# Layer 0's expert products in tiles of 32 columns throughout

## The chip, the core and the metric

The kernel runs on one core of a Trainium2 chip. A core has five engines with queues of their own: TensorE (PE in the profile; its weight loads stand apart as PEld) multiplies matrices into PSUM, VectorE (DVE), ScalarE (ACT) and GpSimd (POOL) compute element by element, and SyncE (SP) issues transfers. Sixteen DMA engines move data between device memory and the core. Engines wait for each other by semaphores alone. The metric is the device time of one execution in microseconds.

TensorE holds a stationary operand of up to 128 rows and 128 columns and streams a moving operand past it. Where the stationary operand has only 64 or 32 columns, two or four products that write different column stretches (here: different partitions of a PSUM bank) can stand side by side in the array.

## The reference

A backbone of two layers over 256 latent and 256 context tokens of width 1024. Each layer has a token mixer and then a mixture of experts, all in fp32. What matters here is the mixture of layer 0, which all 512 tokens pass: each token goes to 2 of 16 experts.

```python
out = jnp.zeros((T, D), F32)
for e in range(N_EXPERTS):
    y = (jax.nn.silu(h @ w1[e]) * (h @ w3[e])) @ w2[e]
    out = out + combine[:, e:e + 1] * y
```

`w1` and `w3` are 1024 x 512, `w2` is 512 x 1024; an expert's weights are 6.3 MB in fp32.

## The kernel before

The kernel goes through layer 0's mixer, its routing, its experts (the function `all0` inside `experts`), then layer 1's mixer and experts. The change is in `all0` alone.

An expert has room for 96 tokens (`cap`). The tokens are the stationary operand, the weights are the moving one, 512 columns at a time. The 96 are cut into `ab`, the first 64, and `cc`, the last 32.

- `hidden(e, q)` (lines 872 to 888), q = 0 to 3, multiplies a quarter of the model width, two slices of 128 (`i`), with the matching pieces of `w3` and `w1` (`j`). For the 64 tokens it issues four matmuls of 64 columns into the bank `A` (tile `h` in the profile): j = 0 goes to partitions 0 to 63, j = 1 to 64 to 127. For the 32 tokens it issues four matmuls of 32 columns into the bank `C` (`hc`), one for each pair of `i` and `j`; the two `i` are added later by `both_halves`.
- `middle(e)` (lines 896 to 910) makes the gated hidden values `gg` on ScalarE and VectorE: it copies and adds the halves of `hc` (lines 893, 894, tile `gs`), takes silu (901, 902) and multiplies (905, or 907 for the last two experts).
- Four transposes on TensorE (line 219, tile `gT`) and a copy on ScalarE (1007) turn `gg`.
- `down(e, gT)` (lines 912 to 933) multiplies with `w2`, 128 rows a piece, in two groups `g` of two pieces: four matmuls of 64 columns into the bank `y[0]`, then four of 32 into `y[1]`. Experts 14 and 15 take another branch, with 96 columns.
- `turn_rows` transposes the gathered tokens of a later expert (tile `xt`), and `aside()` slips in small pieces of routing work (some of them with matmuls `sw`).

The order of TensorE is written out by hand: `in_line` gives each matmul an order token, and the loop over `e` places hidden(e+1, 0) between `middle(e)` and the transposes `gT`, hidden(e+1, 1) and `down(e)` behind them, then `xt`, hidden(e+1, 2), `xt`, hidden(e+1, 3). ScalarE and VectorE keep the order of the tokens named "moe". So all three run in program order.

The weights come on SyncE's queue in the order of use (`stream`), through a ring of 30 buffers of 512 KB (`slots`); a piece is issued when the piece that had its buffer has been used (lines 202 and 863). After expert 11's iteration `without(late)` takes out the buffers that later work needs, and ten are left. Tokens are fetched, and results stored to `yD`, over GpSimd's queue. When expert 13 is stored, GpSimd gathers the results of experts 0 to 13 by token (`room`, line 1063), and `fetched` adds them up. The last two experts are added by a matmul. Behind the weights of the last expert SyncE's queue has layer 1's first weights, `in_od_w_in`.

Of the kernel before, what the change touches and what calls it, by code (L numbers as in the profile page):

```python
# [135 lines left out]
def tile_kernel(ctx: ExitStack, tc: tile.TileContext, I, out, stage=99, dbg=None):  # L136
# [48 lines left out]
    def ps(nm, tag="ps"):  # L185
        tag = alias.get(tag, tag)
        pp, n = psums.get(tag) or psums["ps"]
        return pp.tile([P, 512], F32, tag=tag if tag in psums else "ps", name=nm, bufs=n)
# [18 lines left out]
    def inorder(inst, name="last"):  # L207

        tc.stamp_issue_order_token(inst.ins, name)
# [3 lines left out]
    def mm(*args, **kw):  # L213
        inst = nc.tensor.matmul(*args, **kw)  # L214
        if in_line[0]:
            inorder(inst, "line")
# [233 lines left out]
    def moe(l, tiles, cap, ng, x1, pm, pn, hhi=None, hlo=None):  # L450
# [182 lines left out]
        def experts(pe, ysb, rest, spare=None, next_norm=None):  # L633
# [117 lines left out]
            XTe, xe, idt = {}, {}, {}  # L751
# [60 lines left out]
            def all0(rest):  # L812
# [54 lines left out]
                def weights(e, u):  # L867
                    load(place[e, u] + 3)
                    return loaded[e, u]

                hs = {}
                ab, cc = slice(0, 64), slice(64, 96)

                def hidden(e, q):


                    if q == 0:
                        hs[e] = ps("h", "h"), ps("hc", "h")
                    w = [weights(e, u) for u in (ups[q][1], ups[q][0])]
                    A, C = hs[e]  # L880
                    for i in range(2):
                        for j in range(2):
                            mm(A[64 * j:64 * j + 64, :], XTe[e][:, 2 * q + i, ab], w[j][:, i], start=(q + i == 0),
                               stop=(q + i == 4))
                    for i in range(2):
                        for j in range(2):
                            r0 = 64 * i + 32 * j
                            mm(C[r0:r0 + 32, :], XTe[e][:, 2 * q + i, cc], w[j][:, i], start=(q == 0), stop=(q == 3))
# [22 lines left out]
                def down(e, gT):  # L911


                    y = [ps("y", "y") for _ in range(2)]
                    if e > 13:
                        for f in range(4):
                            w = weights(e, 8 + f)
                            for h in range(2):
                                mm(y[h][r], gT[:, f], w[:, h], start=(f == 0), stop=(f == 3))
                        return y  # L920
                    for g in range(2):
                        ws = [weights(e, 8 + 2 * g + i) for i in range(2)]
                        for i in range(2):
                            for h in range(2):
                                mm(y[0][64 * h:64 * h + 64, :], gT[:, 2 * g + i, ab], ws[i][:, h], start=(g + i == 0),
                                   stop=(g + i == 2))
                        for i in range(2):
                            for h in range(2):
                                r0 = 64 * i + 32 * h
                                mm(y[1][r0:r0 + 32, :], gT[:, 2 * g + i, cc], ws[i][:, h], start=(g == 0), stop=(g == 1))  # L930
                    return y
# [49 lines left out]
                for h in range(2):  # L981
                    turn_rows(0, h)
                hidden(0, 0)
                side.append(one_hot0(2, 4, BF16, put))
                turn_rows(1, 0)
                hidden(0, 1)
                turn_rows(1, 1)
                for _ in range(5):
                    aside()
                hidden(0, 2)  # L990
                side.append(ids(2, 4, put))
                for _ in range(2):
# [5 lines left out]
                for e in range(16):  # L998
# [7 lines left out]
                    gT = pe.tile([P, 4, cap], F32, tag="gT", name="gT", bufs=2)  # L1006
# [3 lines left out]
                    else:  # L1010
                        for n in (2, 3):
                            fetched(n, put)
                    y = down(e, gT)
                    if e < 14:
                        o = ysb[:, e % 2, :]
# [492 lines left out]
    with ExitStack() as es:  # L1508
# [237 lines left out]
        for kh in range(2):  # L1746
            w = cp.tile([P, 4, 512], F32R, tag=f"x{kh + 3}", name="wc")
# [79 lines left out]
    with ExitStack() as es:  # L1827
# [81 lines left out]
        for qt in range(2):  # L1909
            qs = slice(qt * 128, qt * 128 + 128)  # L1910
            ob = pA.tile([P, 512], F32, tag="ob", name="ob", bufs=2)
            for h in range(4):
# [18 lines left out]
                for k in range(4):  # L1931
                    mm(oacc[:, 0:128], wT[:, k, :], dv[:, k, h * 128:(h + 1) * 128],
                       start=(k == 0), stop=(k == 3))
# [23 lines left out]
    with tc.tile_pool(name="pT", bufs=1) as pT:  # L1957

        for q in range(4):
            pTs = []  # L1960
            for hp in range(2):
                h = 2 * q + hp
# [20 lines left out]
            for qt in range(2):  # L1983
                for k in range(4):
                    for hp in range(2):
                        mm(acc_o[64 * hp:64 * hp + 64, qt * 128:qt * 128 + 128],
                           nv[:, k, (2 * q + hp) * 64:(2 * q + hp) * 64 + 64], pTs[hp][:, qt, k, :],
                           start=(k == 0), stop=(k == 3))
# [63 lines left out]
```

## Time and profile before

| | us |
|---|---|
| median of 3 runs | 1437.96 |
| lowest and highest run | 1434.01, 1445.67 |
| the profiled execution's own time | 1443.12 |
| its span, first to last instruction | 1441.1 |
| TensorE busy in it | 1267.0 (88%) |
| VectorE, ScalarE, GpSimd busy | 590.1, 425.6, 218.1 |
| bytes moved | 349.22 MB, 242 GB/s on the mean |

The profile is of one execution. Busy time is the time in which an engine had an instruction of the program in work; matmuls overlap in their pipeline, so a busy TensorE can still have time to give. An fp32 matmul shows as two weight loads and two matmul instructions, and the trace counts each. A row of the timeline joins neighbouring instructions of one kind: start, length from the first start to the last end, count. "PEclk" is the granted share of TensorE's full clock. The DMA share is the mean busy share of the 16 engines; it can read a little over 1.

### The profile page before, as it was taken

Reading aid. Unit: us, or ns where it says so; the run is one execution under the profiler, and the core shown is the slowest. Engines: PE = TensorE matmul, PEld = TensorE weight load, DVE = VectorE, ACT = ScalarE, POOL = GpSimd, SP = SyncE. Lnnn points to the kernel's source line nnn. Section 1 sums busy time; section 2 is a strip of 40 time slices with the busy share of each in tenths; the row PEclk is TensorE's granted clock in tenths of the full one; section 3 lists DMA queues with packets and bytes.
Section 4 is the critical chain, followed back from the end, with each engine's and each line's share of the span. In section 5 each row is a group of like instructions: output and inputs, shape, how many; then the busy total and the mean of one; then the engine's idle time right before and its main releaser. Section 6 shows DMA issues by size and latency. Waiting matters only on the chain. (4 is left out here: it accounts for less than half of the span.)

```text
span 1441.1 us, 22145 instructions
## 1 busy us (share of the span) xinstructions
PE 1267.0 (88%) x8700; PEld 687.0 (48%) x8700; DVE 590.1 (41%) x1329; ACT 425.6 (30%) x835; POOL 218.1 (15%) x271
## 2 busy tenths in 40 slices
PE   5999778888989886999999987799998699999975
PEld 0556556666756672222222223776766544433321
DVE  1326846778656632222112238744636611110003
ACT  2753322222223321221222123324637321111102
POOL 0005520333411301111111120310000100000000
PEclk9999989989999967999999996799999799999998
DMA  9687677766783757999998790651442679999554
GB/s 335 209 256 216 179 181 203 174 172 177 183 262 129 248 221 275 369 383 383 380 382 304 256 365 23 147 139 59 146 169 88 208 265 398 400 396 395 222 223 172
DMA packets 240320, 349.22 MB, mean 242 GB/s; under 512 B 96120, under 2 KB 126104, under 8 KB 239952
## 3 DMA queue, kind: packets, MB, share of 16 engines
q1 hardware_dynamic: 226240, 304.72, 62.9%
q0 software_dynamic: 11264, 34.72, 7.4%
q10 hardware_dynamic: 2704, 8.27, 1.6%
q8 instruction: 72, 1.18, 0.3%
q14 instruction: 40, 0.33, 0.1%
HBM read 326.86 MB, written 20.79 MB: 241 GB/s over the span
## 5 line engine op out<-in xcount | busy, mean ns | idle before, releaser
L214 PE MATMUL y<-w,gT 128*64 128x512 f32 (+2 forms) x736 | 163.0, 612 | 2.1 <-ACT gT L698 1.5
L214 PE MATMUL pj<-hh,whi 128*128 128x512 f32 x432 | 150.1, 429 | 0.6 <-ACT hh L224 0.3
L214 PE MATMUL h<-w,XT 128*64 128x512 f32 x512 | 138.6, 614 | 5.1 <-issue 5.1
L224 DVE TENSOR_TENSOR wlo<-w,whi 128x512 fp32r<-128x512 f32 (+1 forms) x104 | 84.7, 828 | 111.5 <-ACT whi L224 107.4
L214 PE MATMUL h<-w,XE 128*64 128x512 f32 x512 | 125.4, 611 | 3.0 <-ACT XE L790 2.5
L224 ACT ACTIVATE whi<-w 128x512 fp32r<-128x512 f32 (+1 forms) x104 | 69.9, 700 | 155.4 <-DMA w<-in_ev_w_in_dram 73.0
L214 PEld LDWEIGHTS pj<-hh,whi 128*128 128x128 f32 x432 | 83.6, 202 | 32.4 <-issue 9.8
L214 PEld LDWEIGHTS y<-w,gT 128*64 128x64 f32 (+2 forms) x736 | 44.9, 131 | 101.7 <-issue 91.4
L214 PE MATMUL pj<-hh,wlo 128*128 128x512 f32 x216 | 89.9, 418 | 2.1 <-DVE wlo L224 2.0
L214 PE MATMUL ada<-w,sT 128*32 128x512 f32 x384 | 69.0, 639 | 16.9 <-DMA w<-in_ada_w_dram 10.0
L214 PE MATMUL hc<-w,XE 128*32 128x512 f32 x512 | 68.2, 605 | 0.1
L214 PEld LDWEIGHTS h<-w,XT 128*64 128x64 f32 x512 | 36.4, 138 | 63.6 <-issue 57.6
L894 DVE TENSOR_TENSOR ysb<-y,ysb 64x512 f32<-64x512 f32 x14 | 9.7, 695 | 139.1 <-ACT ysb L893 139.1
L214 PEld LDWEIGHTS h<-w,XE 128*64 128x64 f32 x512 | 31.3, 137 | 57.1 <-issue 48.1
L806 DVE SCALAR_TENSOR_TENSOR ylo<-y,sw,yhi 128x512 fp32r<-128x512 f32 x16 | 12.0, 751 | 100.7 <-ACT yhi L805 100.7
L214 PEld LDWEIGHTS pj<-hh,wlo 128*128 128x128 f32 x216 | 43.5, 201 | 17.0 <-DVE wlo L224 4.7
L689 DVE TENSOR_TENSOR gg<-gg,h 64x512 f32<-64x512 f32 x16 | 11.1, 691 | 95.0 <-ACT gg L688 95.0
L2024 POOL TENSOR_TENSOR x<-x,fg 128x512 f32<-128x512 f32 x2 | 2.8, 1378 | 284.9 <-ACT sq L2023 284.9
L1020 POOL DMA_DIRECT2D yD<-ysb x28 | 15.1, 545 | 171.7 <-ACT ysb L1016 171.7
L1016 ACT ACTIVATE ysb<-y 128x512 f32<-128x512 f32 x14 | 8.4, 597 | 99.6 <-PE y L214 99.6
L1316 DVE TENSOR_TENSOR pr<-T,X 128x8 f32<-128x8 f32 (+14 forms) x120 | 35.7, 298 | 4.0 <-DMA X<-xs 0.6
L893 ACT ACTIVATE gs<-hc 64x512 f32<-64x512 f32 x16 | 9.4, 588 | 88.7 <-PE hc L214 88.7
(542 smaller groups left out, 2269.1 us busy)
## 6 DMA issues: line engine op xcount, KB each, us to landing
w<-in_moe_w_dram SPq DMA_DIRECT2D x384, 512.0 KB
w<-in_ada_w_dram SPq DMA_DIRECT2D x96, 512.0 KB
w<-in_ev_w_in_dram SPq DMA_DIRECT2D x27, 512.0 KB
w<-in_od_w_in_dram SPq DMA_DIRECT2D x24, 512.0 KB
sD<-wad SPq DMA_DIRECT2D x16, 256.0 KB
w<-in_ev_w_out_dram SPq DMA_DIRECT2D x8, 512.0 KB
w<-in_od_w_out_dram SPq DMA_DIRECT2D x8, 512.0 KB
yD<-ysb POOLq DMA_DIRECT2D x28, 128.0 KB, 5.3
```

The source lines that it names most:

```text
L214: inst = nc.tensor.matmul(*args, **kw)
L224: for inst in (act(hi, src, AF.Copy), V.tensor_tensor(lo, src, hi.bitcast(F32), op=ALU.subtract)):
L689: V.tensor_tensor(gg[64:128], gg[64:128], acc[64:128], op=ALU.mult)
L806: V.scalar_tensor_tensor(lo, y, w, hi.bitcast(F32), op0=ALU.mult, op1=ALU.subtract))
L893: put(act(o, acc[0:64, :], AF.Copy))
L894: put(V.tensor_tensor(o, acc[64:128, :], o, op=ALU.add))
L1016: put(act(o[:, 0:512], y[0], AF.Copy))
L1020: nc.gpsimd.dma_start(yD[e * cap:e * cap + 64, hs_], o[64 * h:64 * h + 64, 0:512])
L1316: V.tensor_tensor(pr[:, :, 0:t], T[:, 0:t, :].rearrange("p s j -> p j s"), X[:, 0:t, t][:, None, :].to_broadcast([P, 8, t]), op=ALU.mult)
L2024: (V if h else G).tensor_tensor(xt_[:, hs], xt_[:, hs], fg[:, hs], op=ALU.mult)
```

## The change

Where a block had four matmuls of 64 columns it now has eight of 32. The first 64 tokens are cut into two stretches of 32 (`b`), so that with `j` (or `h`) there are four products side by side on the same moving operands: the two `b` read the same weight piece. The results go to the same partitions of the same banks as before. The rest of the block was in fours of 32 already.

```diff
 for i in range(2):
     for j in range(2):
-        mm(A[64 * j:64 * j + 64, :], XTe[e][:, 2 * q + i, ab], w[j][:, i], start=(q + i == 0),
-           stop=(q + i == 4))
+        for b in (0, 32):
+            mm(A[64 * j + b:64 * j + b + 32, :], XTe[e][:, 2 * q + i, b:b + 32], w[j][:, i],
+               start=(q + i == 0), stop=(q + i == 4))
...
 for i in range(2):
     for h in range(2):
-        mm(y[0][64 * h:64 * h + 64, :], gT[:, 2 * g + i, ab], ws[i][:, h], start=(g + i == 0),
-           stop=(g + i == 2))
+        for b in (0, 32):
+            mm(y[0][64 * h + b:64 * h + b + 32, :], gT[:, 2 * g + i, b:b + 32], ws[i][:, h],
+               start=(g + i == 0), stop=(g + i == 2))
```

TensorE's order inside one expert, from the transposes of `gg` to the next transposes `xt`, stands so before (output partitions x columns, and the count of matmuls as the program writes them):

```order
L219 MATMUL gT<-cst,gg 128x96 x4
L214 MATMUL h<-w,XE 64x512 x4
L214 MATMUL hc<-w,XE 32x512 x4
L214 MATMUL y<-w,gT 64x512 x4
L214 MATMUL y<-w,gT 32x512 x4
L214 MATMUL y<-w,gT 64x512 x4
L214 MATMUL y<-w,gT 32x512 x4
L219 MATMUL xt<-cst,xe 128x96 x4
```

And the same place in the changed kernel:

```order
L219 MATMUL gT<-cst,gg 128x96 x4
L214 MATMUL h<-w,XE 32x512 x8
L214 MATMUL hc<-w,XE 32x512 x4
L214 MATMUL y<-w,gT 32x512 x24
L219 MATMUL xt<-cst,xe 128x96 x4
```

Nothing stands in another place: between the transposes the width no longer alternates, and there are 36 matmuls where there were 24. The order on the other engines and on their queues is the same in both kernels.

## Rows read from the trace of the kernel before

**Rows 1.** Windows: busy us (instructions) of each engine, PEclk, DMA share, GB/s.

```profile
560.00:760.00 200.00, 199.90 (x1194) 54.93 (x1192) 46.38 (x100) 40.22 (x71) 32.20 (x52) 1.00 1.04 381
760.00:840.00 80.00, 78.90 (x476) 22.78 (x472) 17.88 (x31) 18.38 (x33) 14.54 (x25) 1.00 0.81 279
840.00:866.00 26.00, 18.21 (x80) 5.28 (x78) 9.73 (x11) 6.18 (x9) 5.65 (x6) 0.96 1.03 390
```

**Rows 2.** Waits of TensorE from 560 to 860: total us, times, longest.

```profile
PE h L214 <- DMA w<-in_moe_w_dram: 0.5, 1, 0.5
```

**Rows 3.** Timeline of TensorE, one expert: start us, length us, engine, line, operation.

```profile
640.94 1.94 PE L214 MATMUL h<-w,XE 128*64 128x512 f32 x8
...
643.80 0.55 PE L219 MATMUL xt<-cst,xe 96*128 96x96 f32 x4
644.28 1.94 PE L214 MATMUL h<-w,XE 128*64 128x512 f32 x8
646.15 1.07 PE L214 MATMUL hc<-w,XE 128*32 128x512 f32 x8
...
650.07 0.55 PE L219 MATMUL gT<-cst,gg 96*128 96x96 f32 x4
650.56 1.94 PE L214 MATMUL h<-w,XE 128*64 128x512 f32 x8
...
659.15 0.55 PE L219 MATMUL xt<-cst,xe 96*128 96x96 f32 x4
```

**Rows 4.** Timeline of TensorE in slits, so that each pass stands alone: down.

```profile
653.42 0.65 PE L214 MATMUL y<-w,gT 128*64 128x512 f32 x2
653.90 0.60 PE L214 MATMUL y<-w,gT 128*64 128x512 f32 x2
654.33 0.60 PE L214 MATMUL y<-w,gT 128*64 128x512 f32 x2
654.76 0.60 PE L214 MATMUL y<-w,gT 128*64 128x512 f32 x2
655.29 0.64 PE L214 MATMUL y<-w,gT 128*32 128x512 f32 x4
655.74 0.61 PE L214 MATMUL y<-w,gT 128*32 128x512 f32 x4
656.28 0.65 PE L214 MATMUL y<-w,gT 128*64 128x512 f32 x2
```

**Rows 5.** Timeline of TensorE in layer 1, where all is 64 wide.

```profile
1306.97 5.37 PE L214 MATMUL h<-w,XT 128*64 128x512 f32 x24
```

**Rows 6.** Timeline of weight loads beside rows 4.

```profile
655.28 0.16 PEld L214 LDWEIGHTS y<-w,gT 128*32 128x32 f32 x8 [0.81 <-issue]
```

**Rows 7.** The tile `hc`: duration of one in ns, minimum/median/maximum.

```profile
L214 PEld LDWEIGHTS hc<-w,XE x512: 106/108/110, 560.3 to 857.2; 128*32 128x32 f32 x171
```

**Rows 8.** Timeline of ScalarE and VectorE beside rows 3: `middle`.

```profile
647.28 0.59 ACT L893 ACTIVATE gs<-hc 64x512 f32<-64x512 f32 x1 [5.56 <-PE hc L214]
...
649.34 0.68 DVE L905 TENSOR_TENSOR gg<-gg,gs 32x512 f32<-32x512 f32 x1
```

**Rows 9.** Timeline of SyncE's issues (`w2`: L863), and expert 11's down on TensorE.

```profile
741.50 4.92 SPq L863 DMA_DIRECT2D w<-in_moe_w_dram  x4
...
809.91 4.16 SPq L863 DMA_DIRECT2D w<-in_moe_w_dram  x4
...
785.39 5.80 PE L214 MATMUL y<-w,gT 128*64 128x512 f32 x32
```

**Rows 10.** Timeline at the end of layer 0's experts.

```profile
837.16 1.01 POOL L1063 DMA_INDIRECT room<-yD,idx  x1 [5.37 <-DMA yD<-ysb]
...
854.81 6.11 SPq L202 DMA_DIRECT2D w<-in_od_w_in_dram  x4
...
864.49 0.63 ACT L224 ACTIVATE whi<-w 128x512 fp32r<-128x512 f32 x1 [4.97 <-DMA w<-in_od_w_in_dram]
...
867.01 0.69 DVE L894 TENSOR_TENSOR gs<-hc,gs 64x512 f32<-64x512 f32 x1
```

## What I predict, before the changed kernel has run

> **What bounds the kernel now.** I read the busy time by stretches first, since the page's shares average over stages with different limits. Layer 0's experts run from about 557 to 882 us. From 560 to 760 TensorE is busy 199.90 of 200 us at the full granted clock, 1.00, and the DMA engines are taken at a share of 1.04: two resources are full at once [rows 1]. So the question is which of them gives way first. The waits of that stage say TensorE: in 300 us it waits for an expert's weights once, for 0.5 us [rows 2]. The weights are there long before they are used. The four `moe_w2` pieces of expert 11 are issued from 741.50 on and used from 785.39, 44 us later [rows 9]. Later the ring of buffers is cut down (`without(late)` after e = 11), and then the DMA engines wait for TensorE: from 760 to 840 their share is 0.81 [rows 1], and the four pieces of expert 13 are issued only at 809.91 [rows 9].
>
> A busy TensorE is not one at its peak, so I looked at what it does inside one expert [rows 3] and inside one block [rows 4]. One fp32 matmul shows as two instructions, and each takes one slot, which I call a pass. Passes on different columns of the array run together: two of 64 columns, or four of 32.
>
> - In layer 1, where 64-wide follows 64-wide without end, 24 instructions are 12 passes and take 5.37 us [rows 5]. The first pass is followed after 0.48 and the last one is seen for 0.60, so ten steps share 5.37 - 0.60 - 0.48 = 4.29: **0.429 us a pass**.
> - In layer 0 the width changes all the time. One block is four 64-wide passes and two 32-wide ones, and its starts stand at 653.42, 653.90, 654.33, 654.76, 655.29, 655.74 and, for the next block, 656.28 [rows 4]: 0.48, 0.43, 0.43, 0.53, 0.45, 0.54 (the last two 0.453 and 0.543 to the third place), together **2.86 us** where six steady passes are 2.57.
>
> So each change of width costs: the pass before it is 0.10 to 0.11 longer, as the array runs empty, and the pass after it 0.05 (64 wide) or 0.024 (32 wide), as its first weights are not loaded ahead.
>
> **The change part by part.** It removes the width changes inside a block and between blocks that follow each other. It adds instructions: a 64-wide pair becomes four of 32, on the same two weight pieces, so the hidden products have 12 matmuls in a block where 8 stood. No other engine's instructions, no transfer and no buffer changes.
>
> What a pass of four costs in a long row, no row of before shows, since no more than two such passes stand together. The nearest rows: two passes of four are 0.45 apart [rows 4], of which 0.024 is the first one's weight load, by the same reckoning that gives 0.48 = 0.43 + 0.05 for a pair. The weights of the second pass are out of the way meanwhile: eight loads start at 655.28 and are over 0.16 us later, while the first four matmuls run until 655.93 [rows 4, 6]. So I take 0.429, and 0.453 as the other end.
>
> What follows a run of such blocks (the transposes `xt`, `gT`, the small `sw`) is 128 columns wide, so a run still ends with 0.543 and begins with 0.453. A run of n passes then takes 0.453 + 0.429 (n - 2) + 0.543. There are three kinds of run:
>
> - **After `gT`, 18 passes** (one hidden block, two of down; 14 times): now 650.56 to 659.15 = 8.59 [rows 3], then 7.86. 0.73 each, 10.2 in all.
> - **Six passes between transposes** (22 times until expert 13's down is done): now 640.94 to 643.80 = 2.86 [rows 3], then 2.71. 0.15 each, 3.3 in all.
> - **Twelve passes before `gT`** (hidden 3 of one expert, hidden 0 of the next; 11 times until there): now 644.28 to 650.07 = 5.79 [rows 3]. By passes alone it would be 5.29. But `gT` needs `gg`, and that is a chain on ACT and DVE which begins when `hc` of the first block ends: at 646.15 + 1.07 = 647.22 [rows 3] ScalarE starts (647.28), DVE is done at 649.34 + 0.68 = 650.02, `gT` starts at 650.07 [rows 3, 8]. Those 2.85 us stay. Today the second block covers them almost exactly; afterwards it is over some 0.35 us too early, and TensorE waits. Only the first block's part is won, 0.13 each, 1.5 in all.
>
> TensorE has then finished expert 13's down **15.0 us** earlier (10.2 + 3.3 + 1.5; 14, 22 and 11 runs). The counts are those of TensorE's order of instructions.
>
> Does that reach the end? Until the ring is cut, the DMA engines are full and can't go faster; TensorE eats into its lead. It would be some 13 us ahead of today around 785, and the lead there is 44 us from issue to use, so it holds. After that the transfers follow TensorE, and their idle part of 760 to 840, (1.04 - 0.81) / 1.04 x 80 = 17.7 us, is room enough for 15.0. The stage's end hangs on a chain that starts from expert 13: its rows are written, GpSimd gathers them from 837.16 on after waiting for that write, and the DMA engines are full from then (1.03 from 840 to 866 [rows 1]); in that queue stands layer 1's first weight, issued at 854.81 and landed at 864.49; DVE, in program order, waits for its split, so that `gs` of expert 15 comes at 867.01 [rows 10]. This chain starts 15.0 us earlier and is as long as before. The few tenths that hidden products of expert 15 win behind it are lost in it. From there on nothing changes but the date.
>
> The sum against the profiled execution's own 1443.12 us (span 1441.1) is 1428.1. The median of the runs, 1437.96, lies 5.2 below that execution, so I forecast 1437.96 - 15.0 = **1423 us**.
>
> **The rivals.**
>
> 1. *A pass of four is dearer in a long row.* The runs counted above hold 14 x 18 + 22 x 6 + 11 x 12 = 516 passes. If every one stays at 0.453, it costs 0.024 more; in the twelve-pass runs the wait for `gg` swallows it, so 384 x 0.024 = 9.2 us are lost and 5.8 remain: 1432. For it: it is the only distance that is seen. Against: the first pass of a pair has the same excess, and there it is gone from the second on.
> 2. *The other side: weights of the next four can't be loaded under the running four.* A load of 32 columns takes 0.108 [rows 7]; exposed in each pass it gives 0.537. 516 x 0.108 = 56 us, less the 15 won and less 11 x 0.35 hidden behind `gg`: 37 us slower, 1475. From 15.0 / 516 = 0.029 more a pass, that is from 0.458 us on, the change loses. Against it: the loads of the second pass lie beside the first four matmuls [rows 4, 6], and layer 1's pairs, which all use the full 128 rows, hold 0.429 [rows 5]. The Trainium skill's page "TensorE: Matmul & The Clock Gate", Part 3, says that weight loads overlap with running matmuls only where their row groups differ; all four tiles here take all rows, so by that rule this rival would come true. The trace disagrees, as far as two passes show.
> 3. *Transfers or a later wait keep part of it.* If the cut ring of buffers, or the gathers at 837, don't move by the full amount, a part of the gain is waited away behind them; if it is half, 7.5 us remain: 1430. For it: the DMA engines are full before and after that hole [rows 1]. Against: the hole is 17.7 us.
> 4. *`gg` doesn't hold back.* If the chain on ACT and DVE were shorter, the twelve-pass runs would win 0.5 each and not 0.13: 11 x 0.37 = 4 more, 1419. Against: from 647.28 to 650.02 it is instructions of ACT and DVE, none of which the change touches [rows 8].
> 5. *It doesn't do what it says*: two tiles read the same weights as moving operand, which no row of before shows; if they took turns the h passes would double, far beyond 1475. I give it little: the pairs read one stationary operand for two tiles with no sign of such a cost [rows 4, 5].
>
> **How the numbers follow.** Forecast 0.60; rival 1 0.12; rival 2 with rival 5 0.08; rival 3 0.13; rival 4 0.07. The range must leave out no more than 0.2: from 1415 (rival 4 and the runs' own spread, 1434 to 1446 before) to 1437 (rivals 1 and 3 with the same spread). One per cent, about what a measurement can tell from no change here, is 14.4 us, and my 15.0 lies just beyond it. So a little over half of the forecast (0.60) counts as faster, with nearly all of rival 4 and a part of its neighbours: 0.52. Within 1%: 0.40. Slower: 0.08.
>
> **What would show it.** In the profile of the changed kernel: `y` runs of 17 or 18 passes with starts 0.43 apart and the run after `gT` at 7.86 us; six-pass runs at 2.71; TensorE waiting about 0.35 us for DVE `gg` before `gT`, a dozen times; a DMA share still full until about 775, then a shorter hole; layer 1's first weight landing 15 us earlier. I am wrong if starts stand at 0.45 or 0.54, if TensorE waits for `w` in the middle of the stage, or if the run after `gT` is short but the landing hasn't moved.

## The result and the profile after

| | before | after |
|---|---|---|
| median, us | 1441.97 (7 runs) | 1425.49 (7 runs) |
| lowest and highest run, us | 1434.01, 1447.28 | 1422.08, 1432.62 |
| the profiled execution's own time, us | 1443.12 | 1432.62 |
| its span, us | 1441.1 | 1430.7 |
| TensorE busy in it, us | 1267.0 (88%) | 1251.3 (87%) |
| matmul instructions in it | 8700 | 9436 |

The changed kernel takes 0.9893 of the time of before, with a 95% interval of 0.9859 to 0.9927: faster by 15.4 us, give or take 4.9, where 15.0 were forecast. It issues 736 more matmul instructions and 736 more weight loads, and is faster for it.

The windows of after answer to [rows 1]; the columns are the same.

```profile
560.00:740.00 180.00, 177.82 (x1624) 56.87 (x1620) 43.98 (x94) 38.55 (x68) 29.19 (x47) 1.00 1.04 378
740.00:780.00 40.00, 39.37 (x364) 12.58 (x360) 8.71 (x17) 9.62 (x17) 9.37 (x17) 1.00 1.04 381
760.00:840.00 80.00, 77.39 (x660) 25.94 (x660) 20.10 (x33) 19.90 (x34) 20.24 (x30) 1.00 0.97 363
```

Two things are new. TensorE, which was busy 199.90 of 200 us, now has gaps: 2.2 us in the first 180. And the hole in the transfers is nearly closed: their share is still full from 740 to 780, and from 760 to 840 it is 0.97 where it was 0.81. By the reckoning of the prediction, (1.04 - 0.97) / 1.04 x 80 = 5.4 us of idle transfers are left of 17.7.

Next is TensorE in one expert of after; it answers to [rows 3].

```profile
639.47 1.92 PE L214 MATMUL h<-w,XE 128*32 128x512 f32 x16
641.22 1.04 PE L214 MATMUL hc<-w,XE 128*32 128x512 f32 x8
...
645.12 0.55 PE L219 MATMUL gT<-cst,gg 96*128 96x96 f32 x4 [0.29 <-DVE gg L906]
```

The run after `gT` is whole in the expert before this one: it begins at 627.94 and the transposes `xt` behind it stand at 635.80. A run of six passes follows.

```profile
627.94 1.92 PE L214 MATMUL h<-w,XE 128*32 128x512 f32 x16
629.68 1.04 PE L214 MATMUL hc<-w,XE 128*32 128x512 f32 x8
630.54 5.33 PE L214 MATMUL y<-w,gT 128*32 128x512 f32 x48
635.80 0.55 PE L219 MATMUL xt<-cst,xe 96*128 96x96 f32 x4
636.28 1.92 PE L214 MATMUL h<-w,XE 128*32 128x512 f32 x16
638.99 0.55 PE L219 MATMUL xt<-cst,xe 96*128 96x96 f32 x4
```

The run of 18 passes takes 635.80 - 627.94 = 7.86 us where it took 8.59, the run of six 638.99 - 636.28 = 2.71 where it took 2.86, and the run of twelve, up to `gT`, 645.12 - 639.47 = 5.65 where it took 5.79.

The weight loads in a run of after follow (PEld is TensorE's weight load; answers to [rows 6]).

```profile
645.60 0.16 PEld L214 LDWEIGHTS h<-w,XE 128*32 128x32 f32 x8
646.05 0.13 PEld L214 LDWEIGHTS h<-w,XE 128*32 128x32 f32 x4 [0.30 <-issue]
646.48 0.13 PEld L214 LDWEIGHTS h<-w,XE 128*32 128x32 f32 x4 [0.30 <-issue]
646.91 0.13 PEld L214 LDWEIGHTS hc<-w,XE 128*32 128x32 f32 x4 [0.30 <-issue]
```

The eight loads at the start serve the first two passes. From then on four loads, 0.13 us together, stand in each step of 0.43 us, under four matmuls that run. No step is longer for them. At 646.91 the products pass from the bank `h` to the bank `hc`, in the same step of 0.43: the change of bank, which went along with each change of width in before, costs nothing by itself.

The waits of TensorE from 560 to 860 (total us, times, longest) answer to [rows 2]:

```profile
PE sc L214 <- DVE gs L895: 8.9, 1, 8.9
PE gT L219 <- DVE gg L906: 3.5, 11, 0.4
...
PE h L214 <- DMA w<-in_moe_w_dram: 0.2, 1, 0.2
```

The 3.5 us in 11 waits for `gg` are new; the weights still hardly ever make TensorE wait. The first line is the end of the stage, which in before lies beyond 860 (9.0 us there).

That end, in the rows that answer to [rows 10]:

```profile
821.94 1.01 POOL L1065 DMA_INDIRECT room<-yD,idx  x1 [5.02 <-DMA yD<-ysb]
...
848.46 0.63 ACT L224 ACTIVATE whi<-w 128x512 fp32r<-128x512 f32 x1 [4.86 <-DMA w<-in_od_w_in_dram]
...
850.98 0.70 DVE L895 TENSOR_TENSOR gs<-hc,gs 64x512 f32<-64x512 f32 x1
```

The first gather comes 15.2 us earlier, the split of layer 1's first weight (`whi`, the first operation on that weight after its landing) 16.0, `gs` of expert 15 16.0. But the stage doesn't begin at the same moment in each execution: the first product of expert 0 starts at 556.99 in before and at 557.18 in after, and between 551 and 562 in the experiments. So from here on I measure from that first product.

| | first product, us | to end of expert 13's down | to first gather | to split of layer 1's weight |
|---|---|---|---|---|
| before | 556.99 | 272.0 | 280.2 | 307.5 |
| after | 557.18 | 257.0 (-15.0) | 264.8 (-15.4) | 291.3 (-16.2) |

The span of the profiled execution fell by only 10.4 us, though. Most of the other 5.8 is lost in layer 1: from the split to layer 1's first expert product it is 289.2 us in before and 294.5 in after. Two places of that stretch hold nearly all of it, with the same work in each. First before:

```profile
930.00:960.00 30.00, 27.37 (x158) 23.78 (x157) 15.25 (x21) 9.38 (x19) 8.68 (x8) 0.94 0.69 176
1062.00:1090.00 28.00, 26.00 (x142) 14.27 (x141) 19.86 (x63) 21.80 (x54) 0.00 (x0) 0.94 0.20 75
```

Then after:

```profile
914.00:946.00 32.00, 28.55 (x156) 24.61 (x157) 15.33 (x21) 8.87 (x17) 8.07 (x7) 0.89 0.64 162
1048.00:1079.00 31.00, 29.24 (x145) 15.65 (x143) 20.37 (x63) 22.11 (x54) 0.00 (x0) 0.83 0.20 68
```

The clock granted was 0.89 and 0.83 where it had been 0.94 twice, and the two stretches took 2 and 3 us more. Whether the change does this or the execution is the question of the third experiment.

### The profile page after: what moved, and what is told of

Its sections match the earlier page's. It is cut to its first block, busy times and chain, and to the rows that moved or that the text cites. A ratio compares the mean times of both kernels' runs of the same rounds, so it can differ in the third digit from the quotient of the medians.

```text
span 1430.7 us, 23616 instructions
## 1 busy us (share of the span) xinstructions
PE 1251.3 (87%) x9436; PEld 693.1 (48%) x9436; DVE 592.2 (41%) x1329; ACT 425.6 (30%) x835; POOL 218.9 (15%) x271
## 5 line engine op out<-in xcount | busy, mean ns | idle before, releaser
L214 PE MATMUL y<-w,gT 128*32 128x512 f32 (+2 forms) x960 | 155.9, 601 | 2.1 <-ACT gT L698 1.5
L214 PE MATMUL h<-w,XE 128*32 128x512 f32 x1024 | 124.1, 603 | 2.7 <-ACT XE L790 2.5
L214 PEld LDWEIGHTS y<-w,gT 128*32 128x32 f32 (+2 forms) x960 | 48.7, 120 | 89.3 <-issue 75.5
L214 PE MATMUL ada<-w,sT 128*32 128x512 f32 x384 | 70.9, 663 | 17.3 <-DMA w<-in_ada_w_dram 10.4
L214 PEld LDWEIGHTS h<-w,XE 128*32 128x32 f32 x1024 | 28.1, 110 | 55.7 <-issue 47.0
L214 PEld LDWEIGHTS hc<-w,XE 128*32 128x32 f32 x512 | 16.0, 110 | 40.0 <-issue 30.6
```

## The experiments

My theory: the width changes cost TensorE time that nothing else fills, both halves of the change win their share, and the gain passes through to the end. The rivals are that one half does all, that something other than the width change is won, and that what is left after the change is bound by something else than I think. All ratios are against the kernel before; times within the stage are counted from the first product of expert 0.

**Only the hidden products.**

```diff
 for i in range(2):
     for j in range(2):
-        mm(A[64 * j:64 * j + 64, :], XTe[e][:, 2 * q + i, ab], w[j][:, i], start=(q + i == 0),
-           stop=(q + i == 4))
+        for b in (0, 32):
+            mm(A[64 * j + b:64 * j + b + 32, :], XTe[e][:, 2 * q + i, b:b + 32], w[j][:, i],
+               start=(q + i == 0), stop=(q + i == 4))
```

> Only the hidden products are cut into 32 columns; down keeps its pairs of 64. Theory (the cost is the change of width: 0.10 to 0.11 us of running empty before it, 0.024 or 0.05 of weight load behind it; a pass costs 0.429 either way): runs of six passes 2.71 us as in the changed kernel, twelve-pass runs 5.65, held by gg; runs after gT 8.43, as the three changes of width in and around down stay. TensorE is 14 x 0.15 + 22 x 0.15 + 11 x 0.13 = 7 us earlier at the end of expert 13's down; time 0.5% below the kernel before. Rival (the four narrow tiles are faster in themselves, whatever their neighbours): the gain goes by the passes changed, two thirds of them in hidden: 10 us.

Ratio 0.9961 (0.9939 to 0.9983). The stage is 6.9 us shorter up to the split of layer 1's weight and 6.8 up to the end of expert 13's down, where the theory said 7 and its rival 10. The timeline of TensorE, the run after `gT` and the transposes behind it:

```profile
607.81 1.92 PE L214 MATMUL h<-w,XE 128*32 128x512 f32 x16
609.55 1.04 PE L214 MATMUL hc<-w,XE 128*32 128x512 f32 x8
610.52 5.80 PE L214 MATMUL y<-w,gT 128*64 128x512 f32 x32
616.25 0.55 PE L219 MATMUL xt<-cst,xe 96*128 96x96 f32 x4
```

8.44 us, 0.15 less than before: the hidden block alone. The last pass of `hc`, with the 64-wide `y` behind it, is dear again: `y` begins 0.97 after `hc`, and in after 0.86.

**Only the down products.**

```diff
 for i in range(2):
     for h in range(2):
-        mm(y[0][64 * h:64 * h + 64, :], gT[:, 2 * g + i, ab], ws[i][:, h], start=(g + i == 0),
-           stop=(g + i == 2))
+        for b in (0, 32):
+            mm(y[0][64 * h + b:64 * h + b + 32, :], gT[:, 2 * g + i, b:b + 32], ws[i][:, h],
+               start=(g + i == 0), stop=(g + i == 2))
```

> Only down is cut into 32 columns; the hidden products keep pairs of 64 for the first 64 tokens. Theory of the change of width: six-pass runs stay at 2.86 us and twelve-pass runs at 5.80; runs after gT 8.01, since four of their changes of width go. 14 x 0.58 = 8 us earlier at the end of expert 13's down, 0.55% below the kernel before, more than the hidden part alone though down has half as many changed passes. Rival (by the passes changed): 5 us.

Ratio 0.9944 (0.9917 to 0.9970), the stage 8.4 us shorter up to the split and 7.7 up to the end of expert 13's down, where the theory said 8 and its rival 5. The same place on TensorE:

```profile
628.87 1.94 PE L214 MATMUL h<-w,XE 128*64 128x512 f32 x8
...
631.62 5.33 PE L214 MATMUL y<-w,gT 128*32 128x512 f32 x48
636.88 0.55 PE L219 MATMUL xt<-cst,xe 96*128 96x96 f32 x4
```

8.01 us, 0.58 less than before; fourteen times that is 8.1. The six-pass runs stay as they were (2.87). So the halves add up: 6.9 + 8.4 = 15.3, and both together bring 16.2 in the profile of after and 15.6 in its second one, below. Neither half does it alone.

**The changed kernel once more.** Nothing is edited against after.

> The changed kernel again on this chip, as the measure for the other three. Theory: ratio 0.989, runs of 7.86, 2.71 and 5.65 us, 15 us earlier at the end of expert 13's down. What layer 1 gains or loses (the profiled execution lost some 6 us there at a lower granted clock) is chance: it should come out otherwise here.

Ratio 0.9889 (0.9857 to 0.9921). To the split the stage is 15.6 us shorter than before. From the split to layer 1's first expert product it takes 289.0 us, where before had 289.2 and the first profile of after 294.5. The two stretches of layer 1 take 30 and 28 us here, as in before:

```profile
918.30:948.30 30.00, 26.70 (x154) 23.17 (x155) 15.24 (x22) 9.42 (x19) 9.09 (x8) 0.94 0.71 175
1050.30:1078.30 28.00, 25.86 (x148) 14.34 (x147) 20.15 (x63) 21.97 (x54) 0.00 (x0) 1.00 0.22 75
```

The 5.3 us lost in layer 1 don't come back in this execution of the same kernel, so they are not the change's. The two half changes say the same: from the split to layer 1's first expert product the kernel with the hidden products cut has 285.9 us, the one with down cut 294.7. This profile's own time is only 11.7 us below that of before, since its first product came 3.9 us later, ahead of everything that the change touches. In the stage itself it lost something too. Its windows of the first blocks of expert 0:

```profile
561.00:566.00 5.00, 5.00 (x28) 1.25 (x28) 0.00 (x0) 0.00 (x0) 0.00 (x0) 0.60 1.02 381
566.00:572.00 6.00, 6.00 (x55) 1.74 (x53) 2.43 (x5) 0.49 (x1) 0.00 (x0) 1.00 1.03 398
```

The clock was 0.60 for the first 5 us, and the first block lasted 4.71 us instead of 4.02 in the first profile. That 0.7 is the difference between the two profiles at the end of expert 13's down: 14.4 and 15.0 us less than before.

**The widths kept, the changes made fewer.** Down takes its four pieces at once: first all 64-wide products, then all 32-wide ones. Against before:

```diff
-for g in range(2):
-    ws = [weights(e, 8 + 2 * g + i) for i in range(2)]
...
+ws = [weights(e, 8 + f) for f in range(4)]
+for f in range(4):
+    for h in range(2):
+        mm(y[0][64 * h:64 * h + 64, :], gT[:, f, ab], ws[f][:, h], start=(f == 0), stop=(f == 3))
+for f in range(4):
+    for h in range(2):
+        r0 = 64 * (f % 2) + 32 * h
+        mm(y[1][r0:r0 + 32, :], gT[:, f, cc], ws[f][:, h], start=(f < 2), stop=(f > 1))
```

> The kernel before with nothing cut narrower: only down's order is changed, all eight 64-wide passes first and then all four 32-wide ones, so that each down has one change of width where it had three. If the change of width is what costs, a run after gT takes 2.86 + 0.48 + 6 x 0.429 + 0.53 + 0.453 + 2 x 0.429 + 0.543 = 8.30 us against 8.59, 0.29 x 14 = 4 us less. If it was the narrower tiles that gained, nothing.

Ratio 0.9960 (0.9932 to 0.9988). The run after `gT`:

```profile
617.32 1.94 PE L214 MATMUL h<-w,XE 128*64 128x512 f32 x8
...
620.18 5.51 PE L214 MATMUL y<-w,gT 128*64 128x512 f32 x32
625.62 0.55 PE L219 MATMUL xt<-cst,xe 96*128 96x96 f32 x4
```

8.30 us, as worked out: one way to 32 columns and back less, 0.29 less, with as many instructions as before and no tile narrower. Up to the end of expert 13's down that makes 3.7 us (fourteen times 0.29 is 4.0, and 0.3 went in the first block: 4.61 us, 4.29 in before), up to the split 3.4. So it is the change of width that costs, not the 64 columns. It is not the change of bank either, which costs nothing in after.

**Fill the wait for `gg`.** Rival 4 said that the twelve-pass runs could win more if the chain on ScalarE and VectorE didn't hold them. In this kernel the transposes of expert e + 2's tokens stand where TensorE waits, ahead of `gT`. Against after:

```diff
     hidden(e + 1, 0)
+    for h in range(2):
+        turn_rows(e + 2, h)
...
-turn_rows(e + 2, 0)
 hidden(e + 1, 2)
-turn_rows(e + 2, 1)
```

> The changed kernel with both transposes xt of an expert moved in front of gT, so that they fill TensorE's wait for gg, and down, hidden 2, hidden 3 and hidden 0 stand in one run of 36 passes where no routing work lies between. By passes: 0.453 + 34 x 0.429 + 0.543 = 15.58 us, eight transposes about 0.71, gT 0.48: 16.8 us an expert against 17.7, so about 0.9 x 13 = 12 us less of TensorE. Theory A (TensorE still sets the pace): 10 to 12 us faster than the changed kernel. Theory B (in the changed kernel the transfers are nearly full: the share is 1.04 until 780 and 0.92 in the hole that is left, 5 us of idle in all): 5 us at most, and TensorE waits for w before the end of the stage.

Ratio 0.9882 (0.9854 to 0.9910): as after, within what can be told. On TensorE it does what it was meant to do:

```profile
630.88 1.92 PE L214 MATMUL h<-w,XE 128*32 128x512 f32 x16
...
646.47 0.88 PE L219 MATMUL xt<-cst,xe 96*128 96x96 f32 x8
647.18 0.49 PE L219 MATMUL gT<-cst,gg 96*128 96x96 f32 x4
```

The waits for `gg` are gone, `xt` and `gT` share one break in the run, and 36 passes follow each other without a longer one: 646.47 - 630.88 = 15.59 us. From `gT` to `gT` an expert takes 16.7 us, in after 17.7. By passes that would be some 12 us, but at the end of expert 13's down TensorE is only 2.7 us ahead of after. Two of its waits say where most of that went:

```profile
PE xt L219 <- DMA xe<-hD,idt: 6.1, 1, 6.1
PE h L214 <- DMA w<-in_moe_w_dram: 0.8, 1, 0.8
```

Expert 2's tokens are wanted earlier than they arrive, once, for 6.1 us, and behind that wait the granted clock is low (0.63 from 576 to 582). From expert 3 on TensorE wins 9.3 us on after, some 3 more than the wait took, and up to the split of layer 1's weight the stage is 288.3 us long, 3.0 less than in after. So neither expectation held cleanly: the theory was right on TensorE and wrong on what reaches the end, and its rival had the size right, but the wait was for tokens, with 0.8 us for weights.

**The same without that wait.** For e = 0 the two `turn_rows` stay at their old places. Against the kernel just described:

```diff
     hidden(e + 1, 0)
-    for h in range(2):
-        turn_rows(e + 2, h)
+    if e:
+        for h in range(2):
+            turn_rows(e + 2, h)
...
+if e == 0:
+    turn_rows(2, 0)
 hidden(e + 1, 2)
+if e == 0:
+    turn_rows(2, 1)
```

> The run with the transposes in front of gT lost 6.1 us in a wait for the tokens of expert 2 in the first iteration, and won 9.3 us of TensorE from expert 3 on. Here expert 2's transposes stay where they were. Theory A (TensorE sets the pace): no such wait, the stage 10 us shorter than in the changed kernel, ratio about 0.982. Theory B (the transfers set it, full at 1.04 until 780 in the changed kernel already): TensorE waits for w or for tokens instead, and the ratio stays at 0.987 to 0.988.

Ratio 0.9857 (0.9815 to 0.9900), between the two forecasts; the interval holds both. The 6.1 us are gone, and a new wait is there, at 773 to 781. TensorE's waits:

```profile
PE hc L214 <- DVE gs L895: 4.0, 1, 4.0
PE h L214 <- DMA w<-in_moe_w_dram: 1.8, 2, 1.3
```

ScalarE at that place (ACTq is its issue of a transfer; in brackets the idle time ahead and what ended it):

```profile
779.67 0.35 ACTq L337 DMA_DIRECT2D xn<-in_norm_g_dram  x1
780.12 0.59 ACT L894 ACTIVATE gs<-hc 64x512 f32<-64x512 f32 x1 [10.41 <-DMA w<-in_moe_w_dram]
```

ScalarE's queue holds the issue of a small transfer for layer 1. By the profile it has to wait for a weight piece, and ScalarE is idle for 10.4 us until the issue is through. For the first 4.5 of them there was nothing to do, as `hc` was done only at 774.2; the other 5.9 `gs` of expert 12 is held in the queue behind the issue. TensorE waits 4.0 us for `gs`, and its clock falls:

```profile
780.00:800.00 20.00, 18.51 (x148) 6.18 (x152) 6.74 (x11) 4.41 (x8) 2.02 (x4) 0.83 0.85 305
```

At the transposes `gT` of expert 11, ahead of this wait, TensorE was 7.5 us ahead of after; at those of expert 12 it is 1.1. Up to the split the stage is 289.7 us long, 1.6 less than in after. The ratios of this kernel and of after overlap; that it beats after is not shown.

**Take passes away from TensorE.** In the second and third quarter of layer 0's hidden products the 32-token products are left out. That is 27 us of passes, with every transfer kept. Against after:

```diff
-for i in range(2):
+for i in range(2 if q in (0, 3) else 0):
     for j in range(2):
         r0 = 64 * i + 32 * j
```

> The changed kernel without the 32-token products of the second and third quarter of the model width in layer 0 (so its output is not the reference's); every transfer stays. Four passes less an expert: by passes alone 16 x 1.7 = 27 us less. It shows what pace the transfers can keep. Theory A: most of it comes. Theory B: the stage is no more than some 10 us shorter than the changed kernel's, and TensorE waits for w many times.

Ratio 0.9812 (0.9766 to 0.9859). The stage up to the split is 287.1 us long: 27 us of TensorE's work less, and 4.2 us shorter than in after. TensorE now waits for weights:

```profile
PE h L214 <- DMA w<-in_moe_w_dram: 16.7, 15, 3.3
PE y L214 <- DMA w<-in_moe_w_dram: 4.5, 4, 1.4
```

And the transfers no longer have a hole before 800:

```profile
740.00:780.00 40.00, 29.31 (x260) 8.66 (x256) 6.38 (x12) 6.28 (x12) 7.13 (x13) 1.00 1.04 382
780.00:800.00 20.00, 18.54 (x168) 5.60 (x160) 6.74 (x11) 4.56 (x8) 2.08 (x4) 1.00 1.04 395
```

The share is 1.04 from 800 to 820 too, and 0.96 from 820 to 840. So the transfers of this stage need about 287 us to bring layer 1's first weight, in the order and with the buffers that they have; up to there the stage took 307.5 in before and takes 291.3 in after. The change has brought it from 20 us above that floor to 4. That explains why the two kernels ahead of it won so little: up to that weight a further saving on TensorE can give those 4 us. That the wait for tokens and the wait behind ScalarE's queue come from transfers being so near their floor fits this, but no run takes that apart.

It is not the floor of the whole stage, though. In this kernel, and in none of the others, VectorE has `gs` of expert 15 ahead of its part of the split (`wlo`). First after, with its last down products:

```profile
849.12 0.69 DVE L224 TENSOR_TENSOR wlo<-w,whi 128x512 fp32r<-128x512 f32 x1 [4.44 <-ACT whi L224]
...
855.36 9.51 PE L214 MATMUL y<-w,gT 128*96 128x512 f32 x16 [0.58 <-ACT gT L1009]
```

Its `gs`, shown above, comes at 850.98, behind `wlo`. Then this kernel:

```profile
836.66 0.69 DVE L895 TENSOR_TENSOR gs<-hc,gs 64x512 f32<-64x512 f32 x1 [6.47 <-ACT gs L894]
...
838.93 0.69 DVE L224 TENSOR_TENSOR wlo<-w,whi 128x512 fp32r<-128x512 f32 x1
...
840.43 9.74 PE L214 MATMUL y<-w,gT 128*96 128x512 f32 x16
```

TensorE's wait for `gs`, 8.9 us in after, is 1.5 here. The last of these products ends 299.2 us after the first product, in after 307.7: 8.5 us earlier, and the median of the runs, 1415.15, is 10 us below that of after. That is what theory B said, some 10 us at most and many waits for weights. How much of what lies beyond the 4 us came from the other order and how much from the passes left out, no run takes apart.

## Why the prediction was right, point by point

- **A steady pass of four.** Taken as 0.429 us, with 0.453 as the other end. The first and third start in the weight loads above lie 646.48 - 645.60 = 0.88 apart, 0.45 + 0.43, and every later step is 0.43. Rival 1 is out: with 17 steps of 0.453 and the exit of 0.543 the run after `gT` would have taken 8.24. Its price in the prediction was a little too high: by the formula there the first and the last pass of a run are dear already, so 14 x 16 + 22 x 4 = 312 passes and not 384 would have cost 0.024 more, 7.5 us. In rival 2, too, the first pass of each of the 47 runs was counted although its first load is exposed already, which makes 5 us of the 56 at most.
- **The exit of a run** stays at 0.543, as reckoned: 0.453 + 16 x 0.429 + 0.543 = 7.86, measured 7.86; for six passes 2.71, measured 2.71.
- **Weight loads under running matmuls.** Rival 2 is out: four loads lie in each step of 0.43, and the 36-pass run of the fifth experiment here, 15.59 us, leaves no room for an exposed load. By the rule of the Trainium skill's page "TensorE: Matmul & The Clock Gate", Part 3, that loads overlap with running matmuls only where row groups differ, each step would have been near 0.54 (an estimate, 0.429 + 0.108); all these tiles use all rows, and the measurement decides against that rule here. The same part, a paragraph earlier, also has a load pulled ahead when it goes to a background weight buffer, and the steps of 0.43 don't contradict that.
- **Two tiles on one moving operand.** Rival 5 is out by the same rows.
- **The `gg` chain.** It does hold the twelve-pass runs: 11 waits of about 0.3 us, forecast as a dozen of 0.35. From the end of `hc` at 641.22 + 1.04 = 642.26 to `gT` at 645.12 it is 2.86 us, 2.85 before. Rival 4 is out. That there was gain to be had by filling the wait, as rival 4's price suggested (4 us), the two kernels with moved transposes bear out on TensorE (9.3 and 7.5 us), but hardly at the end.
- **The sum on TensorE**: forecast 15.0 at the end of expert 13's down, measured 15.0, and 14.4 in the second profile with its slow first block. The time alone, 15.4 with 4.9 either way, excludes the 5.8 of rival 1, the 7.5 of rival 3 and the loss of rival 2, but not the 19 of rival 4; that one the traces exclude.
- **Does it reach the end?** Yes, and this was the tightest step. The hole in the transfers was said to be room enough for 15.0, with 17.7 us; 12.3 of it are used up by after, in the window of [rows 1]. How near that was to the limit the other kernels show. With the transposes moved (the fifth experiment) TensorE was 17.8 us ahead of before at the end of expert 13's down, and all of it reached the split, 19.2 us earlier. With passes left out it was 22.9 ahead, and the split came 20.4 earlier: somewhere near 20 us the part of rival 3 that speaks of transfers comes true. The forecast gave both numbers, 17.7 and 15.0, and did not say how near they lie.
- **The date of layer 1's first weight.** Forecast 15.0 earlier, measured 16.2 from the first product (15.6 in the second profile). The gather came 15.4 earlier, and from the gather to the split it is 26.5 us instead of 27.3. Why that piece became shorter isn't settled; nothing was tried on it.
- **The starting point.** The saving was taken from 1437.96, a median of three runs. Seven runs have 1441.97; from there 15.0 less would have been 1427. The median of after, 1425.49, lies between 1423 and that. So that 1423 came within 3 us is in part luck: the start was taken 4 us too low, and the split came a little earlier than forecast. The sum against the profiled execution, 1428.1, was missed by 4.5: that execution lost 5.3 in layer 1, nearly all of it in the two stretches at a lower clock, which the third experiment shows to be no effect of the change.

## What to carry to other kernels

Where the array is packed with narrow tiles, count the changes of width, not the tiles: a kernel that alternates 64 and 32 columns can be faster with more and narrower matmuls, or with the same ones in another order, as long as the weights are loaded under the running ones. Before a saving on one full engine is believed, measure what the next full resource leaves: here transfers with a share of 1.04 and a hole of 17.7 us left room for this change and little for the one after it. A kernel that leaves work out and keeps every transfer shows that floor in one run, if the order of the remaining work stays as it was: here it did not at the end, and the floor holds only up to there.

## What the runs showed of the hardware that I had not expected

- There and back between 64 and 32 columns costs 0.29 us, with two passes of 32 columns in between or with four: three such ways in a run of 18 passes (the way in from 128 columns and the way out to them together stand for the last way back) make 18 x 0.429 + 3 x 0.29 = 8.59, two make 8.30. Without any it is 7.86, where only the way from and to 128 columns is left, 0.14. The Trainium skill's page "TensorEngine Tiling (Array Packing)", Key Properties, says that a change of the tiling mode drains TensorE, without a price; the traces agree, and this is the price here.
- A clock that isn't full makes profiled executions of one kernel differ by as much as a third of this change: 5.5 us in layer 1 between the two profiles of after, at 0.89 and 0.83 in two stretches of the slower one, 0.94 and 1.00 in the other. A span alone would have told of 10.4 us gained where the stage had gained 16.2.
- The issue of one small transfer on a compute engine's queue, while it waits, holds the engine's work behind it: in the sixth experiment 5.9 us on ScalarE, and 4.0 us of waiting on TensorE.
